# Router logits from rows not yet normed, first norm's scale and shift on gathered tokens, mixer's end in fixed order, last norm's rows from columns

## The chip, the cores and the metric

The kernel runs on one core of one Trainium2 chip. The metric is the device time of one execution in microseconds (us); the median of three executions stands for a kernel. The engines are TensorE (PE), VectorE (DVE), ScalarE (ACT), GpSimd (POOL) and SyncE (SP, which here issues nearly all transfers).

## The reference

One encoder layer over 256 tokens of width 1024. Everything is float32.

```
y  = token_mixer(x)                       # two attention branches, gates, w_out, b_out
x1 = layer_norm(ALPHA*x + y, ln1_g, ln1_b)
logits = x1 @ w_router + b_router         # 32 experts
top 4 per token, softmax over the 4 -> gates
y2[t] = sum over its 4 experts of gate * (act(x1[t] @ w_up[e] + b_up[e]) @ w_down[e] + b_down[e])
out = layer_norm(ALPHA*x1 + y2, ln2_g, ln2_b)

layer_norm(x, g, b): (x - mean) * rsqrt(var + 1e-5) * g + b
```

All 32 experts have tokens, so the 32 x 12 MB of expert weights are read once.

## The kernel before

**The mixer.** `unit(n)` and the two loops behind it go through 28 slabs of weights (w_in, w_proj_a, w_proj_b, w_out), each of 1 MB in four pieces. `split` makes a high and a low part of each piece (a cast on ACT, a subtraction on DVE or POOL), and `products` takes three matmuls of 256 columns for each 128 rows of depth. The last four slabs are those of w_out: for u = 0 to 3, PE makes columns 256u to 256u+255 of the mixer's output for two blocks of 128 tokens (tt = 0, 1), 24 matmuls each; DVE adds them to `xs` (ALPHA*x + b_out, already there) and takes `bn_stats`. In u = 3 the two token blocks go one after the other (`one_by_one`).

**Norm and router.** For each token block: mean and variance, 1/sqrt, the normed rows `nrm`, eight transposes of 128x128 into PSUM, two copies into `nT`, and eight matmuls of `wrg` (w_router with ln1_g already in it) into `lgq`, four depth groups in four groups of 32 partitions. `sums` adds the four groups into `lgp`. Beside that, POOL (block 0) and DVE (block 1) put ln1_g and ln1_b on the normed rows, which gives `x1`. Then the largest eight logits (`V.max`), the mask `s16` of the top four, the rank of each token in its expert (`rk`, `posm`), and a one-hot matrix `oh` for two experts.

**Experts.** `gather_half` multiplies `x1` with `oh` (16 matmul instructions for each half of the width) and gives the tokens of two experts, in columns, in `xe`. For expert e, `gate_of` and `up_of` (8 steps of depth each, one PSUM bank) and `down_of` run on PE, and their hooks put other small work between two steps: the gather for later experts, the transposes `turn_of`, `gates_for`, and `combine`, which adds an expert's output into the four `acc` banks. The stream of weights is g0 u0, then (g1 d0 u1), (g2 d1 u2) and so on to (g31 d30 u31), d31. Each stands for four transfers of 1 MB; they go in this order through 20 SBUF slots (`SLOTS`, the names `r_...` in the profile). SP issues the transfer into a slot when PE has used up what was there 20 transfers earlier, with at most eight on the way. In a few slots the mixer's own data lies first: `w0` and `w1` hold the split pieces, `xh` and `xl` the mixer's merged rows and later `nrm` and `nT`.

**Order.** In the mixer and the router the framework's scheduler orders each engine's instructions. From the first expert on, the order is that of the code (`manual_schedule`).

**The end.** In `up_of(31)`, four hooks spread the rows ln2_g and ln2_b over 128 partitions: ACT's queue loads the two rows into one partition (`r_tab`), a matmul of one row of depth makes `pr`, ACT copies it to `rows2` (`r_qa`). After expert 31, `final` norms `acc`: three of the four blocks on DVE, block (0, 1) on ACT and POOL, each block then written out by a transfer that SP issues in the order (0, 1), (0, 0), (1, 0), (1, 1).

## Time and profile before

| | |
|---|---|
| median of 3 runs (lowest, highest) | 1185.61 us (1184.1, 1187.65) |
| profiled execution: its time | 1182.13 us |
| its span, first to last instruction | 1180.4 us |
| PE busy | 1095.8 us, 93% |
| DVE, ACT, POOL busy | 274.1, 206.3, 55.0 us |
| moved by the DMA engines | 440.20 MB, mean 373 GB/s |
| mean granted TensorE clock | 0.98 |

The profile gives for each engine what it did when, and what released it after a wait. A matmul instruction is listed with its full latency, and the next one starts before it ends, so a busy PE isn't a PE at its peak; time per instruction in a row of matmuls is the group's time through its count. PE at 93% and DMA at 373 GB/s are means over a mixer (to about 215 us), a router (to about 232 us), 32 experts and a short end.

### The profile page before, as it was taken

What the parts mean: (1) busy time and instruction counts of PE and PEld (TensorE: products, weight loads), DVE (VectorE), ACT (ScalarE), POOL (GpSimd) and SP (SyncE); (2) the same over time, 40 slices, a digit from 0 to 9 for tenths busy, and PEclk for the clock granted to TensorE, in tenths of its full rate; (3) what the DMA queues carried; (4) which work ended last, traced back from release to release, by engine and by line L of the source; (5) the groups of instructions that cost most, each with busy time, mean ns of one, the idle gap of its engine ahead of it and who ended that gap; (6) DMA issues with size and microseconds to landing.
All of it is one profiled execution on the core that took longest, in us unless ns stands there. A gap on an engine that the chain in (4) does not pass through costs nothing.

```text
span 1180.4 us, 14053 instructions
## 1 busy us (share of the span) xinstructions
PE 1095.8 (93%) x5797; PEld 509.1 (43%) x5798; DVE 274.1 (23%) x570; ACT 206.3 (17%) x403; POOL 55.0 (5%) x77
## 2 busy tenths in 40 slices
PE   6989999799999999999999999999999899999883
PEld 6888999633334333333333333333333333333221
DVE  5957457411111111111111101111111111111103
ACT  3556654310001011010000001011000000000011
POOL 1730002200000000000000000000000000000001
PEclk9999999899999999999999989999999999999987
DMA  8765749699999999999999999999999999999971
GB/s 283 260 228 200 253 161 319 227 412 421 421 421 420 421 421 421 421 421 421 421 421 421 421 421 422 422 421 421 421 421 422 421 421 421 421 421 421 421 323 38
DMA packets 86651, 440.20 MB, mean 373 GB/s; under 512 B 7348, under 2 KB 33588, under 8 KB 37462
## 3 DMA queue, kind: packets, MB, share of 16 engines
q1 hardware_dynamic: 85666, 436.45, 91.1%
q0 software_dynamic: 720, 2.62, 0.7%
q8 instruction: 48, 0.79, 0.3%
q10 hardware_dynamic: 196, 0.17, 0.1%
q14 instruction: 21, 0.17, 0.0%
HBM read 438.16 MB, written 1.05 MB: 372 GB/s over the span
## 4 chain that ended last, share of the span: by engine, by line
DMA 56%; PE 22%; DVE 1%; issue 1%; ACT 0%; SPq 0%; ACTq 0%
DMA r_a<-in_w_ex 10%; DMA r_xl<-in_w_ex 8%; DMA r_ob<-in_w_ex 8%; DMA r_s<-in_w_ex 7%; DMA r_v<-in_w_ex 7%; PE pg L605 6%; PE pu L605 6%; DMA r_w<-in_w_ex 5%; PE pd L637 5%; DMA r_gb<-in_w_ex 3%; DMA r_qb<-in_w_ex 3%; DMA r_p<-in_w_ex 3%; PE px L581 2%; PE acc L645 1%; PE acc L681 1%
## 5 line engine op out<-in xcount | busy, mean ns | idle before, releaser
L594 DVE COPY ot<-po 128x256 f32<-128x256 f32 x32 | 13.6, 424 | 508.5 <-PE po L592 508.5
L210 PE MATMUL pt<-r_xh,r_w 128*128 128x256 f32 x512 | 101.0, 296 | 10.5 <-ACT r_w L188 5.8
L210 PEld LDWEIGHTS pt<-r_xh,r_w 128*128 128x128 f32 x512 | 84.8, 201 | 13.0 <-ACT r_w L188 5.5
L189 DVE TENSOR_TENSOR r_w<-r_s,r_w 128x512 fp32r<-128x512 f32 x104 | 72.3, 712 | 42.7 <-ACT r_w L188 42.1
L583 ACT COPY xe<-px 128x512 f32<-128x512 f32 x32 | 18.8, 586 | 356.6 <-PE px L581 349.3
L613 DVE TENSOR_SCALAR gc<-pg 128x512 f32<-128x512 f32 x32 | 22.1, 692 | 246.0 <-PE pg L605 246.0
L188 ACT CAST r_w<-r_s 128x512 fp32r<-128x512 f32 x112 | 66.8, 617 | 62.4 <-PE pt L210 31.7
L210 PE MATMUL pt<-r_xl,r_w 128*128 128x256 f32 x256 | 74.8, 292 | 0.0
L581 PEld LDWEIGHTS px<-oh,x 128*128 128x128 f32 x512 | 61.2, 196 | 28.1 <-issue 15.9
L581 PE MATMUL px<-oh,x 128*128 128x128 f32 x512 | 66.9, 285 | 1.8 <-DVE oh L572 0.9
L645 PE MATMUL acc<-y,ot 64*128 64x512 f32 x256 | 64.3, 621 | 0.7 <-ACT y L640 0.7
L640 ACT COPY y<-pd 128x512 f32<-128x512 f32 x32 | 18.8, 586 | 214.0 <-PE pd L637 214.0
L637 PE MATMUL pd<-r_a,at 128*64 128x512 f32 x224 | 51.3, 597 | 4.6 <-DMA r_a<-in_w_ex 3.9
L630 ACT COPY at<-pa 128x512 f32<-128x512 f32 x32 | 18.8, 586 | 204.5 <-PE pa L628 204.5
L605 PE MATMUL pg<-r_a,xe 128*64 128x512 f32 x224 | 53.2, 613 | 0.0
L210 PEld LDWEIGHTS pt<-r_xl,r_w 128*128 128x128 f32 x256 | 51.7, 202 | 0.1
L605 PE MATMUL pu<-r_a,xe 128*64 128x512 f32 x192 | 46.3, 603 | 2.6 <-DMA r_a<-in_w_ex 2.6
L212 PE MATMUL pt<-r_w,r_xh 128*128 128x256 f32 x256 | 47.6, 285 | 0.7 <-DVE r_w L189 0.7
L793 POOL TENSOR_TENSOR r_qb<-r_qb,r_qa 128x512 f32<-128x512 f32 x1 | 1.7, 1682 | 949.7 <-ACTq L805 949.7
L212 PEld LDWEIGHTS pt<-r_w,r_xh 128*128 128x128 f32 x256 | 40.2, 192 | 2.1 <-DVE r_w L189 1.2
L645 PEld LDWEIGHTS acc<-y,ot 64*128 64x128 f32 x256 | 22.4, 189 | 43.0 <-issue 41.4
L212 PE MATMUL pt<-r_w,r_xl 128*128 128x256 f32 x128 | 36.3, 284 | 0.2 <-DVE r_xl L490 0.2
(269 smaller groups left out, 1365.8 us busy)
## 6 DMA issues: line engine op xcount, KB each, us to landing
r_a<-in_w_ex SPq DMA_DIRECT2D x79, 1024.0 KB, 19.8
r_s<-in_w_ex SPq DMA_DIRECT2D x38, 1024.0 KB, 19.8
r_w<-in_w_ex SPq DMA_DIRECT2D x38, 1024.0 KB, 19.8
r_s<-in_w_in SPq DMA_DIRECT2D x19, 1024.0 KB, 6.5
r_qa<-in_w_ex SPq DMA_DIRECT2D x19, 1024.0 KB, 19.8
r_tab<-in_w_ex SPq DMA_DIRECT2D x19, 1024.0 KB, 19.8
r_qb<-in_w_ex SPq DMA_DIRECT2D x19, 1024.0 KB, 19.8
r_v<-in_w_ex SPq DMA_DIRECT2D x19, 1024.0 KB, 19.8
```

Source lines behind the costliest of these rows:

```text
L188: S.copy(w[:, 0:2], src)
L189: (G if n % 4 == 3 and n >= 80 else V).tensor_sub(w[:, 2:4], src, w[:, 0:2].bitcast(F32))
L210: PE.matmul(os[j], w[:, a + b, c], d[:, k], start=st, stop=sp)
L212: PE.matmul(os[j], d[:, k, c], w[:, a + b], start=st, stop=sp)
L581: PE.matmul(px[:, k], x1[:, tt, (4 * h + k) * P:(4 * h + k + 1) * P], oh[:, tt].rearrange("p a b -> p (a b)"), start=tt == 0, stop=tt == N ...
L583: S.copy(xe[:, 4 * h:4 * h + 4], px)
L605: PE.matmul(pu[h * CAP:(h + 1) * CAP], xe[:, k, i * CAP:(i + 1) * CAP], w(k)[:, h * 512:(h + 1) * 512], start=False, stop=k == KD - 1)
L613: V.tensor_scalar(gc, pg, LIMIT, None, op0=ALU.min)
L630: S.copy(at, pa)
L637: PE.matmul(pd[dh * CAP:(dh + 1) * CAP], at[:, k % 4, k // 4 * CAP:(k // 4 + 1) * CAP], w(k)[:, dh * 512:(dh + 1) * 512], start=k == 0, st ...
L640: S.copy(y, pd)
L645: PE.matmul(o, ot[q, tt], y[q], start=start, stop=stop)
```

## The change

1. **Router.** `wrg` gets its column mean subtracted over all 1024 rows (`csm`, eight more matmuls in `router_parts`), so that logits can be made from rows that aren't centred; 1/sqrt is put on the 32 logits instead of the 1024 columns. The transposes and the logit matmuls then work on `xs`, in four parts of 256 columns, each behind its unit u of w_out.
2. **First norm.** ln1_g and ln1_b no longer go on the rows: `x1` is only normed (on ACT, in place). The gathered tokens get scale and shift as columns in `gather_half`, four activations of 128x128 for one copy of 128x512. The residual for the last norm takes ALPHA*ln1_g through `spread`, and ALPHA*ln1_b as a 33rd row of `bdn`. The loads of g1 and b1 fall away.
3. **Order.** Unit u = 3 and everything to the rank stands in `manual_schedule`.
4. **Last norm.** ln2_g and ln2_b come as columns with `bcol`; they are spread in the hooks of `gate_of(31)`, one expert stage earlier, with a 128x128 identity. `final` is written in another order, and block (0, 1) goes out through ACT's queue, the others through SP's.
5. The register with the largest count is read after expert 3 instead of at the end, and the second half of the first gather uses another PSUM bank.

```diff
         def router_parts():
             ...
+            for k in range(KD):
+                PE.matmul(pl[:, 128:128 + NE], ones, wrg[:, k], start=k == 0, stop=k == KD - 1)
+            V.tensor_scalar(csm, pl[:, 128:128 + NE], -1.0 / D, None, op0=ALU.mult)
+            V.tensor_add(wrg, wrg, csm[:, None].to_broadcast([P, KD, NE]))
...
-        for u in range(4):
-            py = banks()
-            products(py, 96 + 4 * u, 4, (mh, ml), False, u == 3)
-            for tt in range(NT):
-                xq = xs[:, tt, u * 256:(u + 1) * 256]
-                V.tensor_add(xq, py[tt], xq)
-                V.bn_stats(st[:, tt, u], xq)
+        def turned_x(u, tt, xT):
+            tp = pst.tile([P, 2, P], F32, name="pt", tag="tp")
+            for j in range(2):
+                PE.transpose(tp[:, j], xs[:, tt, (2 * u + j) * P:(2 * u + j + 1) * P], ident)
+            S.copy(xT[:, tt], tp)
+        def logits(u, tt, xT):
+            for j in range(2):
+                k = 2 * u + j
+                g = slice(k % 4 * NE, (k % 4 + 1) * NE)
+                if u < 3:
+                    PE.matmul(lgq[g, tt, :P], wrg[:, k], xT[:, tt, j], start=k < 4, stop=k >= 2)
+                else:
+                    PE.matmul(lgp[:, tt], xT[:, tt, j], wrg[:, k], start=False, stop=j == 1)
+            if u == 2:
+                S.copy(lq[:, tt], lgq[:, tt, :P])
+                PE.matmul(lgp[:, tt], lq[:, tt], sums, start=True, stop=False)
+        def normed(tt):
+            ...
+                S.activation(x1[:, tt, c], xs[:, tt, c], AF.Identity, bias=nmr[:, t], scale=ri[:, t])
+        def largest(tt):
+            V.scalar_tensor_tensor(lg[:, tt], lgp[:, tt], ri[:, tt:tt + 1], lgbb, op0=ALU.mult, op1=ALU.add)
+            ...
+        for u in range(3):
+            py = banks()
+            products(py, 96 + 4 * u, 4, (mh, ml), False)
+            for tt in range(NT):
+                summed(u, tt, py)
+                turned_x(u, tt, xTs[u])
+                logits(u, tt, xTs[u])
+        with tc.manual_schedule():
+            ...
+            for i in range(4):
+                quarter(0, i)
+            summed(3, 0, py)
+            stats(0)
+            quarter(1, 0)
+            quarter(1, 1)
+            turned_x(3, 0, xTs[3])
+            normed(0)
+            quarter(1, 2)
+            logits(3, 0, xTs[3])
+            largest(0)
+            quarter(1, 3)
+            summed(3, 1, py)
+            turned_x(3, 1, xTs[3])
+            logits(3, 1, xTs[3])
+            stats(1)
+            normed(1)
+            largest(1)
...
-        S.copy(xe[:, 4 * h:4 * h + 4], px)
+        for k in range(4):
+            f = 41 + 4 * h + k
+            S.activation(xe[:, 4 * h + k], px[:, k], AF.Identity, bias=bcol[:, f + 8:f + 9], scale=bcol[:, f:f + 1])
...
+        def spread(c, m):
+            pr = ps.tile([P, 512], F32, name="pr", tag="m")
+            for k in range(4):
+                PE.matmul(pr[:, k * P:(k + 1) * P], bcol[:, c + k:c + k + 1].to_broadcast([P, P]), m, start=True, stop=True)
+            return pr
...
+                if n == NE - 1:
+                    rows2, fo = part(slot("qa"), 0, 2048, 2), part(slot("qb"), 0, 2048, 2)
+                    def rows(j, dh):
+                        S.copy(rows2[:, j, dh * 512:(dh + 1) * 512], spread(57 + 8 * j + 4 * dh, ident))
+                    for k, a in zip((1, 2, 3, 4), ((0, 0), (0, 1), (1, 0), (1, 1))):
+                        hooks[k] = lambda a=a: rows(*a)
+                gate_of(n, hooks)
...
-                        PE.matmul(pr, ones[0:1], row[:, j, c], start=True, stop=True)
-                        S.copy(rows2[:, j, c], pr)
...
-                nc.sync.dma_start(out[tt * P:(tt + 1) * P, c], o)
+                ((S if (tt, i) == (0, 1) else nc.sync)).dma_start(out[tt * P:(tt + 1) * P, c], o)
```

PE at the border between units u = 0 and u = 1 of w_out, before (`pt` is a unit's PSUM bank, `r_w_112` and `r_w_113` the split pieces, `r_xh` and `r_xl` the merged rows):

```order
L212 MATMUL pt<-r_w_113,r_xl 128x256
L212 MATMUL pt<-r_w_113,r_xh 128x256
L212 MATMUL pt<-r_w_112,r_xh 128x256
L212 MATMUL pt<-r_w_112,r_xl 128x256
L212 MATMUL pt<-r_w_112,r_xh 128x256 x2
```

PE at the same place now (`x_75` is the tile of `xs`):

```order
L211 MATMUL pt<-r_w_113,r_xh 128x256
L211 MATMUL pt<-r_w_112,r_xh 128x256
L211 MATMUL pt<-r_w_112,r_xl 128x256
L211 MATMUL pt<-r_w_112,r_xh 128x256
L495 MATMUL pt<-ident,x_75 128x128 x2
L211 MATMUL pt<-r_w_112,r_xh 128x256
L495 MATMUL pt<-ident,x_75 128x128 x2
L211 MATMUL pt<-r_w_112,r_xl 128x256
L505 MATMUL lgq<-xT,wrg 32x128 x2
L211 MATMUL pt<-r_w_112,r_xh 128x256
L505 MATMUL lgq<-xT,wrg 32x128 x2
L211 MATMUL pt<-r_w_112,r_xh 128x256
```

Between the products of u = 1 now stand the four transposes and four logit matmuls of u = 0; the same happens at the two borders that follow.

PE from the mixer's last product to the first of the rank's matmuls (L561), before:

```order
L534 MATMUL pt<-ident,nrm_2388 128x128 x8
L539 MATMUL lgq<-r_xl,wrg 32x128 x8
L534 MATMUL pt<-ident,r_xh 128x128 x8
L539 MATMUL lgq<-r_xl,wrg 32x128 x8
L549 MATMUL lgp<-sums,lq 128x32 x2
L561 LDWEIGHTS tri_135
L561 MATMUL pt<-s_2399,tri_135 128x32
```

PE at the same place now, with the mixer's last product (L211) ahead and the rank in L592:

```order
L211 MATMUL pt<-r_w_113,r_xh 128x256
L495 MATMUL pt<-ident,x_75 128x128 x2
L507 MATMUL lgq<-wrg,xT 128x32 x2
L592 LDWEIGHTS tri_134
L592 MATMUL pt<-s_2158,tri_134 128x32
```

Of 34 matmuls between the last product and the rank, four are left there.

PE in the up stage of the last expert, before (`pr` is a spread row, `acc` the sum over the experts):

```order
L605 MATMUL pu<-r_w_6225,xe 64x512 x2
L758 MATMUL pr<-r_tab,ones 128x512
L605 MATMUL pu<-r_w_6225,xe 64x512 x2
L758 MATMUL pr<-r_tab,ones 128x512
L605 MATMUL pu<-r_w_6227,xe 64x512 x2
L645 MATMUL acc_2491<-y_6218,ot 128x512
```

PE in the gate stage of the last expert now, two stages ahead of that place:

```order
L641 MATMUL pg<-r_pt,xe 64x512 x4
L725 MATMUL pr<-ident,bcol 128x128 x4
L641 MATMUL pg<-r_p,xe 64x512 x2
L725 MATMUL pr<-ident,bcol 128x128 x4
L641 MATMUL pg<-r_p,xe 64x512 x2
L725 MATMUL pr<-ident,bcol 128x128 x4
L641 MATMUL pg<-r_oa,xe 64x512 x2
L725 MATMUL pr<-ident,bcol 128x128 x4
L641 MATMUL pg<-r_oa,xe 64x512 x2
L664 MATMUL pa<-ident,uc 128x128 x4
```

The up stage of expert 31 now holds only its own products, `combine(30)` and the two transposes of `gates_for(31)`.

## Rows read from the trace of the kernel before

**Rows 1.** Page, 40 slices of the span: what the DMA engines moved.
```profile
GB/s 283 260 228 200 253 161 319 227 412 421 421 421 420 421 421 421 421 421 421 421 421 421 421 421 422 422 421 421 421 421 422 421 421 421 421 421 421 421 323 38
```
**Rows 2.** Windows, router to first expert: us, engines' busy time, clock, DMA share, GB/s.
```profile
222.00:224.00 2.00, 0.71 (x4) 0.53 (x5) 1.49 (x14) 0.00 (x0) 0.00 (x0) 0.62 1.21 377
...
228.00:230.00 2.00, 1.19 (x7) 0.92 (x7) 0.00 (x0) 0.59 (x1) 0.00 (x0) 0.67 0.00 0
...
232.00:234.00 2.00, 2.00 (x12) 0.64 (x10) 0.45 (x2) 1.41 (x4) 0.00 (x0) 1.00 0.00 0
```
**Rows 3.** Timeline from the last product: start us, us, engine, line, operation, [idle before].
```profile
214.23 0.28 PE L212 MATMUL pt<-r_w,r_xl 128*128 128x256 f32 x1
214.35 0.28 PE L212 MATMUL pt<-r_w,r_xh 128*128 128x256 f32 x1
214.67 0.42 DVE L497 TENSOR_TENSOR x<-pt,x 128x256 f32<-128x256 f32 x1
...
216.60 0.35 DVE L524 SCALAR_TENSOR_TENSOR nmr<-mv,ri 128x1 f32<-128x1 f32 x1
...
222.01 0.19 DVE L550 TENSOR_TENSOR lg<-lgp,lgbb 128x32 f32<-128x32 f32 x1 [0.29 <-PE lgp L549]
...
224.55 0.42 DVE L572 TENSOR_TENSOR oh<-io,posm 128x256 f32<-128x256 f32 x1
225.19 3.75 PE L581 MATMUL px<-oh,x 128*128 128x128 f32 x16 [0.93 <-DVE oh L572]
...
229.75 2.02 PE L581 MATMUL px<-oh,x 128*128 128x128 f32 x16 [0.81 <-ACT xe L583]
...
231.94 3.60 PE L605 MATMUL pg<-r_a,xe 128*64 128x512 f32 x16
...
233.87 2.04 SPq L123 DMA_DIRECT2D r_a<-in_w_ex  x2
```
**Rows 4.** Chain that ended last, in its last 53 us: start us, us, what.
```profile
1130.30 4.34 DMA r_tab<-in_ln_g
...
1152.70 0.70 DVE uc L621
...
1155.62 7.11 PE pd L637 x32
```
**Rows 5.** Timeline and a window: first piece of u31, and the last bytes of weights.
```profile
1130.67 1.08 PE L605 MATMUL pu<-r_w,xe 128*64 128x512 f32 x4 [0.34 <-DMA r_w<-in_w_ex]
...
1146.00:1148.00 2.00, 2.00 (x8) 0.49 (x6) 0.00 (x0) 0.59 (x1) 0.00 (x0) 1.00 0.19 78
```
**Rows 6.** Timeline of the last norm's end.
```profile
1168.72 0.78 ACT L792 ACTIVATE r_qb<-acc,nmr,rs 128x512 f32<-128x512 f32 x1 [0.29 <-DVE nmr L786]
...
1171.34 1.59 POOL L794 TENSOR_TENSOR r_qb<-r_qb,r_qa 128x512 f32<-128x512 f32 x1
...
1172.51 0.97 DVE L797 SCALAR_TENSOR_TENSOR r_qb<-r_qb,rs,r_qa 128x512 f32<-128x512 f32 x1
1172.96 2.08 SPq L798 DMA_DIRECT2D out<-r_qb  x4
```
**Rows 7.** Lines by form, 60 to 232 us: xcount, busy us, mean ns, idle before.
```profile
L353 PEld LDWEIGHTS pt<-ones,r_p 128*128 128x128 f32 x16 | 1.9, 192 | 0.0
...
L534 PE MATMUL pt<-ident,nrm 128*128 128x128 f32 x8 | 1.0, 272 | 0.0
...
L539 PE MATMUL lgq<-r_xl,wrg 128*32 128x128 f32 x32 | 1.7, 285 | 0.6 <-ACT r_xl L535 0.5
...
L344 ACT COPY ob<-pv 128x256 f32<-128x256 f32 x4 | 1.5, 374 | 2.9 <-PE pv L343 2.9
...
L548 ACT COPY lq<-lgq 128x128 f32<-128x128 f32 x2 | 0.4, 258 | 0.0
...
L583 ACT COPY xe<-px 128x512 f32<-128x512 f32 x2 | 1.2, 586 | 9.5 <-issue 7.3 <-PE px L581 2.2
```
**Rows 8.** Window in which PE runs the router's constants (L443 to L446).
```profile
152.00:154.00 2.00, 2.00 (x12) 2.00 (x11) 1.27 (x2) 0.62 (x1) 0.00 (x0) 0.50 0.91 285
```

More of the change, by code (lines that the diff above doesn't have):

```diff
@@ L517, in encoder, with stats @@
         zs = small.tile([P, NT], F32, name="zs")
-        for tt in range(NT):
+        V.memset(top, BIG)
+        def stats(tt):
             V.bn_aggr(mv[:, tt], st[:, tt].rearrange("p a b -> p (a b)"))
@@ L547, in encoder @@
-        for tt in range(NT):
-            S.copy(lq[:, tt], lgq[:, tt, :P])
-            PE.matmul(lgp[:, tt], lq[:, tt], sums, start=True, stop=True)
-            V.tensor_add(lg[:, tt], lgp[:, tt], lgbb)
-            V.max(top[:, tt], lg[:, tt])
-            V.tensor_scalar(nv1[:, tt:tt + 1], top[:, tt, 0:1], -1.0, None, op0=ALU.mult)
-            V.memset(top[:, tt, TOPK:], BIG)
+                S.activation(x1[:, tt, c], xs[:, tt, c], AF.Identity, bias=nmr[:, t], scale=ri[:, t])
+        def largest(tt):
+            V.scalar_tensor_tensor(lg[:, tt], lgp[:, tt], ri[:, tt:tt + 1], lgbb, op0=ALU.mult, op1=ALU.add)
+            t8 = small.tile([P, 8], F32, name="t8")
+            V.max(t8, lg[:, tt])
+            V.tensor_copy(top[:, tt, :TOPK], t8[:, :TOPK])
@@ new lines, in encoder, with quarter @@
+        for u in range(3):
[6 more added lines that the diff above has]
+        with tc.manual_schedule():
+            py = banks()
+            pieces = [next_piece(108 + i) for i in range(4)]
+            def quarter(tt, i):
+                products_of(py, pieces[i], i, 4, (mh, ml), False, tt)
+            for i in range(4):
[16 more added lines that the diff above has]
+            largest(1)
+            rk = pst.tile([P, 512], F32, name="pt", tag="tp")
+            for tt in range(NT):
+                o = rk[:, tt * NE:(tt + 1) * NE]
+                for t2 in range(tt):
+                    PE.matmul(o, ones16, s16[:, t2], start=t2 == 0, stop=False)
+                PE.matmul(o, tri16, s16[:, tt], start=tt == 0, stop=True)
+            V.scalar_tensor_tensor(posm.rearrange("p a b -> p (a b)"), rk[:, :NT * NE], 1.0,
+                                   s16.rearrange("p a b -> p (a b)"), op0=ALU.add, op1=ALU.mult)
+            V.tensor_scalar(nv1, top[:, :, 0], -1.0, None, op0=ALU.mult)
+            S.activation(dummy, s16[:, 1, 0:1], AF.Exp, scale=0.0)
@@ L870 @@
     a["lam"] = np.concatenate([a["lambda_q1"], a["lambda_q2"], a["lambda_k1"], a["lambda_k2"]])
-    rows = np.concatenate([a["b_in"], a["subln_g"], a["ln1_g"], a["ln1_b"]]).reshape(-1, P)
+    rows = np.concatenate([a[k] for k in ("b_in", "subln_g", "ln1_g", "ln1_b", "ln2_g", "ln2_b")]).reshape(-1, P)
     wr = a["w_router"].reshape(KD, P, NE).transpose(1, 0, 2).reshape(P, KD * NE)
```

190 lines of the change are left out of this document (80 added, 110 removed).

## Prediction

> **What bounds the kernel now.** I first read what the DMA engines move in 40 slices of the span [rows 1]: from the ninth slice (236 us; 412 GB/s) to the last but two it is 420 to 422 GB/s without a dip, and the first eight slices are far below. So from the first expert on the weight stream sets the pace, and PE, though 93% busy, only follows it. What PE does in an expert costs nothing as long as it gives slots back in time. The end is then set by two places alone: when the stream gets going, and what comes after its last bytes.
>
> **The start of the stream.** Windows of 2 us show the DMA engines at a share of 0.00 at 228 to 230 and again at 232 to 234 us [rows 2]: all 20 slots are full, and the next transfer can be issued only when PE has used the first piece of g0. The timeline gives the steps [rows 3]: last product of the mixer issued at 214.35 and ended at 214.63; one-hot matrix at 224.55; first gather half at 225.19, 3.75 us because TensorE's granted clock is 0.50 by then (0.62 in the mean of 222 to 224, 0.67 in that of 228 to 230, 1.00 at 232 [rows 2]); second half at 229.75, 2.02 us; g0 at 231.94; next transfer issued at 233.87. From the end of the last product to g0 it is 231.94 - 214.63 = 17.3 us. Whatever g0 gains, the whole stream gains.
>
> **After the stream.** The chain that ended last has PE in its last 50 us [rows 4]: at 1130.30 ACT's queue asks for the row ln2_g, which takes 4.34 us to land, and PE stands behind it in u31, with the spread matmuls. u31 ends at 1152.70 (DVE starts on it), d31 starts at 1155.62 and takes 7.11 us. But the first piece of u31 was used at 1130.67, at once on landing, and the last weights had landed by 1148 (78 GB/s are left in 1146 to 1148) [rows 5]. PE thus runs behind its data here, and only here.
>
> **The change, front.** It moves work ahead of the mixer's last product, where PE has no gap, and takes work from behind it. In units of rows 7:
> - Column mean of `wrg`: 8 matmuls, 16 instructions with 128x128 weights; 16 of such cost 1.9 us in L353. They stand beside the router's constants, where the clock is 0.50 [rows 8], so up to 3.8; I take 2.5.
> - 14 of the 16 transposes: 1.0 / 8 = 0.125 us each, 1.8 us.
> - 12 logit matmuls of 32 weight columns, 24 instructions at 1.7 / 32 = 0.053: 1.3 us.
> - 8 instructions with 128 weight columns (sums over the four groups, last logits of block 0) at 0.12: 0.9 us.
> - Waits that are new. At three borders between units PE has three products to do (0.12 us from one issue to the next [rows 3], 0.36 us) and then waits for DVE's addition, which begins 0.32 us after the last product's issue and takes 0.42 [rows 3], then for ACT's copy of the transposes, 0.37 us (L344's form) against some 0.5 us of PE work with its hops. Behind the waiting transposes and logits PE's queue holds all later products. I take 0.55 us a border, 1.6 us; bounds 0 and 3.
>
> Together the last product ends 2.5 + 1.8 + 1.3 + 0.9 + 1.6 = 8.1 us later (5.9 with no wait and the full clock, 10.8 with both worst ends).
>
> Behind the last product now lies: DVE's addition 0.04 us later, the token block's scalars 1.93 us after its start (216.60 - 214.67 [rows 3]; the two transposes, one copy and two logit matmuls fit beside that), then from logits to the one-hot matrix 224.55 - 222.01 = 2.54 us for both blocks, of which block 0's share is done earlier, so I take 2.0; the one-hot matrix and hop 225.19 - 224.55 = 0.64; the gather. Its second half no longer waits for ACT (0.81 us) as it has its own bank. The gather took 3.75 + 2.02; PE idles before it about as long as it did, so I expect part at half clock, 5.2 us (4.0 when all at full clock, 7.5 when none). Sum 0.04 + 1.93 + 2.0 + 0.64 + 5.2 + 0.1 = 9.9 us (8.7 to 12.2) against 17.3: 7.4 us less. **Net, g0 comes 8.1 - 7.4 = 0.7 us later** (from 2.8 earlier to 5.7 later). That is the surprise of this sum: work taken from behind the mixer is put into it nearly at par. The norm's row operations that POOL and DVE lose (L543 to L546) lay beside this path and give nothing.
>
> **The change, tail.** The 4.34 us wait and the spreads leave u31. In g31 there are now four spreads of 8 instructions, 4 x 8 x 0.12 = 3.8 us of PE; the copy of one (0.59 us, L583's form) is done before the next hook. A piece of 1.049 MB takes 2.49 us at 421 GB/s [rows 1], and PE uses some 1.9 for it (3.60 us for two [rows 3], and hops), so it waits at nearly each, as at 1130.67 [rows 5]; over the eight pieces of g31 and d30 it has 8 x 0.55 = 4.4 us to spare, so u31 starts within 0.3 us of its data. With pieces landing from 1130.7 on at 1133.2, 1135.6 and 1138.1, `combine(30)` (1.9 us) behind the third step: 1133.2 + 0.97 + 1.9 + 0.97 = 1137.0 for two pieces, + 1.9 for the third = 1138.9, + 2.4 with `gates_for(31)` = 1141.3. That is 1152.7 - 1141.3 = **11.4 us earlier**. d31 then starts at 1144.2 and ends at 1151.3, and its last piece, there by 1148, is used from 1149.5: the weights aren't late. Were they as late as 1150, 10.9 would remain; were the spare of g31 and d30 half of what I count, 9.5.
>
> **The last norm.** Before, SP's first output waited for POOL, which ended at 1172.93, and the four issues took 2.08 us from 1172.96 [rows 6]; DVE's last block was ready at 1173.48, but its issue was the fourth. Now DVE's three go out as they are ready, and the last is issued at about 1173.3 (relative to the old clock) instead of 1174.6; ACT's block starts with the second square root, 0.3 us before 1168.72. I take **1.5 us** (0.4 to 2.0).
>
> The Trainium skill speaks against that last step: "DMA: Bandwidth & Descriptors", section "Issuing engines are not separate DMA queues", says that transfers issued from several engines end up on the same 16 DMA engines, and that only the sequencer's issue time is saved. By it, the step would give one issue of 2.08 / 4 = 0.5 us, and the forecast would be 1.0 us higher; the trace has the order of the wait to add to it, which the rule doesn't speak of.
>
> **At nothing:** the register read after expert 3 (SP has up to eight transfers on the way); the residual's spreads at experts 17 and 19 and the wider gate row (PE's spare in the stream); four activations instead of one copy, 4 x 0.26 against 0.59 us [rows 7], since PE goes on with other steps meanwhile. If ACT's cover is gone, that costs 0.4 us for each half gather, once at g0.
>
> **Sum.** Against the profiled execution: 1182.1 + 0.7 - 11.4 - 1.5 = 1169.9 us. The median of the runs before lies 3.5 us above that execution, so 1173.4, I say 1173.5.
>
> **The rivals.**
> - *The front gains too.* No waits at the borders, full clock in the gather: 2.8 us earlier instead of 0.7 later, 1170. For it: products before overlap weight loads fully, so small matmuls between them may be partly free. Against: PE in order, and each wait stands in its queue.
> - *The clock falls at the borders.* Stretches in which PE had gaps pulled the clock to 0.50 in two places [rows 2, 8]; new waits at three borders plus the thin stretch behind the mixer could do the same. The first gather half lost 3.75 - 2.02 = 1.7 us by it [rows 3]; two such losses in the mixer and the gather wholly at half clock (7.5 instead of 5.2) are 2 x 1.7 + 2.3 = 5.7 us on top, 1179.2.
> - *The tail returns only part.* If g31's spreads block each other on the one PSUM bank and PE doesn't catch up by u31, 4 us remain there: 1177.5.
> - *Slower than before.* One mechanism: at half clock from the first border to the last product, the 24 x 2 x 3 products of 0.12 us cost 17.3 us more, 1190.8. It decides once g0 comes more than 12.9 us later, the 11.4 + 1.5 of the tail. Against: the waits that I count are under a tenth of a unit's 5.8 us.
> - *It doesn't do what it says*, that is, the rows still come late: the order shows no spread left in u31, so I give it nothing of its own.
>
> **How the numbers follow.** Forecast 0.62, front gains 0.14, clock 0.13, part of the tail 0.08, slower 0.03. The range from 1167.5 to 1180 takes in the first four nearly whole and the bounds 2.8 earlier and 5.7 later of g0. A measurement can tell 0.3%, 3.6 us, from no change, so faster means under 1182.0: all of the forecast, of the front's gain and of the tail's part, and most of the clock's case: 0.93; same 0.04; slower 0.03.
>
> **What would show it.** In the profile after: no `r_tab<-in_ln_g` in the chain; u31 without a wait beyond its pieces, DVE's `uc` about 11 us sooner after the first piece of u31 than 22.0 us; g0 within 3 us of 231.94, with the mixer's last product at about 222.7 and the DMA share still at zero for some us ahead of g0; GB/s flat at 421 after. If g0 moves by more than 5 us, my prices at the borders are wrong; if u31 ends less than 9 us earlier, the spare of g31 is.

## The result, and the profile after

The changed kernel takes 1170.53 us (median of 4 executions, 1166.54 to 1173.10) against 1184.86 us before (4 executions, 1181.37 to 1187.65): ratio 0.9878, 95% interval 0.9833 to 0.9922. In a second session it was 1172.65 us (6 executions) against 1183.89 (11): 0.9897, interval 0.9878 to 0.9916. The prediction was 1173.5 us. It was right in sum; in the front it was right for a reason that held only at equal clock.

The profiled execution of after took 1173.09 us, with a span of 1171.3. Set against the span of 1180.4 before, it divides like this (us; the marks are the first instruction of g0, DVE's first `uc` of u31, the last combine of PE, and the end of the span):

| stretch | before | after | difference | predicted |
|---|---|---|---|---|
| start to g0 | 231.94 | 236.06 | +4.1 | +0.7 |
| g0 to `uc` of u31 | 920.76 | 909.59 | -11.2 | -11.4 |
| `uc` to last combine | 10.75 | 10.75 | 0 | 0 |
| last combine to end | 16.95 | 14.90 | -2.05 | -1.5 |

The tail and the outputs came as the prediction had them. The front did not, and its 4.1 us fit this profile's place above the median: the front turned out to have more than one length (below).

**The front.** The timeline of after from the mixer's last product to g0, as in [rows 3]: start us, us, engine, line, operation, [idle before].

```profile
224.30 0.28 PE L211 MATMUL pt<-r_w,r_xh 128*128 128x256 f32 x1
224.92 0.42 DVE L514 TENSOR_TENSOR x<-pt,x 128x256 f32<-128x256 f32 x1
225.39 0.44 PE L495 MATMUL pt<-ident,x 128*128 128x128 f32 x2 [0.82 <-DVE x L514]
226.29 0.63 PE L507 MATMUL lgq<-wrg,xT 128*128 128x32 f32 x4 [0.46 <-ACT xT L496]
228.20 0.18 PE L592 MATMUL pt<-s,tri 128*128 128x32 bf16 x1 [1.24 <-DVE s L550]
229.16 6.74 PE L615 MATMUL px<-oh,x 128*128 128x128 f32 x32 [0.78 <-DVE oh L605]
...
236.06 3.60 PE L641 MATMUL pg<-r_a,xe 128*64 128x512 f32 x16
...
237.99 0.33 SPq L123 DMA_DIRECT2D r_a<-in_w_ex  x1
```

From DVE's last addition to g0 it is 236.06 - 224.92 = 11.1 us, where [rows 3] have 231.94 - 214.67 = 17.3. The gather's 32 products stand in one row now, without ACT between the halves; but they take 6.74 us. The windows say why (columns as in [rows 2]: busy time of PE, its weight loads, DVE, ACT, POOL, then clock, DMA share, GB/s):

```profile
230.00:232.00 2.00, 2.00 (x11) 2.00 (x11) 0.00 (x0) 0.00 (x0) 0.00 (x0) 0.50 1.01 426
232.00:234.00 2.00, 2.00 (x11) 2.00 (x11) 0.00 (x0) 1.02 (x3) 0.00 (x0) 0.50 1.00 422
234.00:236.00 2.00, 2.00 (x14) 1.87 (x14) 0.00 (x0) 0.55 (x3) 0.00 (x0) 0.68 0.13 53
236.00:238.00 2.00, 2.00 (x12) 0.70 (x10) 0.11 (x1) 1.85 (x6) 0.00 (x0) 1.00 0.00 0
```

The granted clock is 0.50 in the gather. The DMA engines run dry shortly after 234, ahead of g0, and stand until after 238. Further up, the timeline of PE shows a larger loss:

```profile
147.99 0.50 PE L209 MATMUL pt<-r_xh,r_w 128*128 128x256 f32 x2 [1.48 <-DVE r_w L189]
...
151.22 3.46 PE L440 MATMUL pt<-wrg,ones 128*128 128x32 f32 x16
```

and two windows the clock there:

```profile
150.00:154.00 4.00, 4.00 (x20) 4.00 (x21) 1.86 (x3) 0.00 (x0) 0.00 (x0) 0.50 0.76 248
154.00:160.00 6.00, 6.00 (x30) 6.00 (x30) 1.91 (x4) 1.71 (x3) 0.00 (x0) 0.50 0.03 10
```

PE waits 1.48 us for DVE (which waits for the output projection's bias), and the clock then stays at 0.50 from 149.9 to 160.2 us: 10.2 us, where before had 3.4 us of it, from 150.8 to 154.2, behind a wait of 1.58 us:

```profile
150.00:154.00 4.00, 4.00 (x22) 3.83 (x22) 3.16 (x7) 1.24 (x2) 0.00 (x0) 0.60 0.48 145
```

The new column mean (L440) lies inside the stretch of after and takes 3.46 us.

The borders between the mixer's last units, by contrast, show no wait at all on PE:

```profile
208.82 0.28 PE L211 MATMUL pt<-r_w,r_xh 128*128 128x256 f32 x1
208.96 0.44 PE L495 MATMUL pt<-ident,x 128*128 128x128 f32 x2
209.15 0.36 PE L211 MATMUL pt<-r_w,r_xh 128*128 128x256 f32 x1
209.35 0.38 PE L495 MATMUL pt<-ident,x 128*128 128x128 f32 x2
209.49 0.36 PE L211 MATMUL pt<-r_w,r_xl 128*128 128x256 f32 x1
209.86 0.41 PE L505 MATMUL lgq<-xT,wrg 128*32 128x128 f32 x4
210.20 0.50 PE L211 MATMUL pt<-r_w,r_xh 128*128 128x256 f32 x2
210.54 0.28 PE L211 MATMUL pt<-r_w,r_xl 128*128 128x256 f32 x1
210.75 0.41 PE L505 MATMUL lgq<-xT,wrg 128*32 128x128 f32 x4
```

No row has an idle time; the scheduler wove the transposes and logits between products of the next unit. Still a border costs time: DVE's additions for the three units start at 201.08, 208.48 and 215.88, 7.40 us apart, and before at 197.18, 202.85 and 208.61, 5.7 to 5.8 apart. So a border costs 1.6 to 1.7 us: the transposes and logits themselves, about 1.0 us by these rows, and the rest in small steps between unlike products (0.37 us from 209.49 to 209.86, where two products in a row stand 0.12 apart).

**The tail.** DVE's `uc` in the timeline:

```profile
1145.65 0.69 DVE L657 TENSOR_SCALAR uc<-pu 128x512 f32<-128x512 f32 x1 [0.59 <-PE pu L641]
```

and the chain that ended last in this stretch (start us, us, what), as in [rows 4]:

```profile
1122.23 20.87 DMA r_xl<-in_w_ex
1143.15 1.08 PE pu L641 x4
1144.60 1.03 PE pu L641 x4
1148.58 7.11 PE pd L673 x32
```

No `r_tab<-in_ln_g` any more: what u31 waits for is its last weight piece, which landed at 1143.1. From the first use of u31's weights to `uc` it is now 1145.65 - 1134.98 = 10.7 us, and 22.0 before [rows 4, 5]. In before, more than the row's load and the spreads lay in those 22.0 us:

```profile
1134.77 2.04 PE L758 MATMUL pr<-r_tab,ones 1*128 1x512 f32 x2 [3.02 <-DMA r_tab<-in_ln_g]
...
1138.00:1140.00 2.00, 2.00 (x4) 0.50 (x2) 0.00 (x0) 0.00 (x0) 0.00 (x0) 0.50 0.99 406
```

In the wait of 3.02 us for the row the granted clock fell to 0.50, from 1133.9 to 1144.1 us; u31 of after has no such stretch. The outputs, as in [rows 6]:

```profile
1163.18 1.59 POOL L839 TENSOR_TENSOR r_qb<-r_qb,r_qa 128x512 f32<-128x512 f32 x1
...
1163.68 3.46 SPq L843 DMA_DIRECT2D out<-r_qb  x3
...
1164.81 0.38 ACTq L843 DMA_DIRECT2D out<-r_qb  x1
...
1166.02 0.75 DVE L842 SCALAR_TENSOR_TENSOR r_qb<-r_qb,rs,r_qa 128x512 f32<-128x512 f32 x1
```

SP's first output leaves at 1163.68, 1.1 us before POOL's block is done.

### The profile page after: what moved, and what is told of

Same layout as the page of the kernel before. It is cut to its first block, busy times and chain, and to the rows that moved or that the text cites. A ratio compares the mean times of both kernels' runs of the same rounds, so it can differ in the third digit from the quotient of the medians.

```text
span 1171.3 us, 14250 instructions
## 1 busy us (share of the span) xinstructions
PE 1100.1 (94%) x5853; PEld 522.7 (45%) x5854; DVE 274.2 (23%) x573; ACT 238.8 (20%) x505; POOL 47.6 (4%) x71
## 4 chain that ended last, share of the span: by engine, by line
DMA 50%; PE 44%; DVE 4%; issue 1%; ACT 1%; SPq 0%; DVEq 0%; ACTq 0%
DMA r_p<-in_w_ex 10%; DMA r_w<-in_w_ex 10%; DMA r_qb<-in_w_ex 10%; PE pt L209 9%; PE pu L641 9%; DMA r_a<-in_w_ex 8%; DMA r_gb<-in_w_ex 8%; PE pg L641 7%; PE pd L673 6%; PE pt L211 3%; PE px L615 3%; PE acc L681 3%; DMA r_xl<-in_w_ex 2%; DVE r_w L189 1%; PE sc L275 1%
## 5 line engine op out<-in xcount | busy, mean ns | idle before, releaser
L619 ACT ACTIVATE xe<-px,bcol 128x128 f32<-128x128 f32 x128 | 48.1, 456 | 355.6 <-PE px L615 355.6
L209 PE MATMUL pt<-r_xh,r_w 128*128 128x256 f32 x512 | 103.5, 300 | 8.3 <-ACT r_w L188 5.4
L209 PEld LDWEIGHTS pt<-r_xh,r_w 128*128 128x128 f32 x512 | 87.0, 206 | 11.1 <-ACT r_w L188 5.1
L211 PE MATMUL pt<-r_w,r_xh 128*128 128x256 f32 x256 | 49.8, 289 | 0.6 <-DVE r_w L189 0.6
L211 PEld LDWEIGHTS pt<-r_w,r_xh 128*128 128x128 f32 x256 | 40.6, 191 | 3.1 <-issue 1.5
L211 PE MATMUL pt<-r_w,r_xl 128*128 128x256 f32 x128 | 36.6, 286 | 0.2 <-DVE r_xl L486 0.2
```

The costliest lines, as they stand in the source:

```text
L209: PE.matmul(os[j], w[:, a + b, c], d[:, k], start=st, stop=sp)
L211: PE.matmul(os[j], d[:, k, c], w[:, a + b], start=st, stop=sp)
L619: S.activation(xe[:, 4 * h + k], px[:, k], AF.Identity, bias=bcol[:, f + 8:f + 9], scale=bcol[:, f:f + 1])
```

## The experiments

Each kernel ran beside the kernel before on the same chip; the times are medians, the ratios have their 95% interval. The runs e1 to e4 shared one chip, after_again and e5 to e7 another, e8 to e11 a third; the last four had no run of the changed kernel beside them, so they are set against it by their ratios to before. To take the first 130 us out (they differ by up to 5 us between the profiles), the table also gives the time from the products with `rq` (L354; L359 before; 135.38 in the profile of before) to g0, read from each kernel's profile.

| kernel | median (executions) | ratio to before | `rq` to g0 | half clock, 146 to 160 | DVE's last addition to g0 | g0 to end |
|---|---|---|---|---|---|---|
| before | 1182 to 1185 | 1 | 96.6 | 3.4 | 17.3 | 948.5 |
| after | 1170.53 (4) | 0.9878 | 101.6 | 10.2 | 11.1 | 935.2 |
| after_again | 1172.65 (6) | 0.9897 | 101.8 | 10.2 | 9.9 | 937.0 |
| e1_tail_alone | 1172.74 (4) | 0.9923 | 96.4 | 3.4 | 17.2 | 937.8 |
| e2_front_alone | 1180.99 (10) | 0.9993 | 101.6 | 10.2 | 11.0 | 946.7 |
| e3_old_outputs | 1170.99 (5) | 0.9919 | 95.6 | none | 9.9 | 938.5 |
| e4_late_read | 1166.85 (4) | 0.9876 | 95.8 | none | 10.4 | 937.5 |
| e5_no_mean | 1166.06 (5) | 0.9848 | 95.0 | none | 11.0 | 934.9 |
| e6_early_bias | 1168.19 (4) | 0.9872 | 94.5 | none | 10.4 | 937.2 |
| e7_no_idle | 1168.85 (4) | 0.9870 | 99.5 | 10.2 | 9.0 | 935.5 |
| e8_both | 1165.67 (6) | 0.9861 | 92.8 | none | 9.0 | 936.1 |
| e9_sum_first | 1164.71 (5) | 0.9859 | 94.5 | none | 10.4 | 936.8 |
| e10_all | 1167.72 (6) | 0.9869 | 91.5 | none | 9.0 | 938.6 |
| e11_best | 1164.56 (5) | 0.9846 | 90.8 | none | 8.2 | 935.3 |

### The tail alone

The kernel before, with the spreads from columns in g31 instead of the row loads in u31:

```
-                    for j, src in enumerate((ln2g, ln2b)):
-                        S.dma_start(row[:, j], src[None, :])
...
+                    for k, a in zip((1, 2, 3, 4), ((0, 0), (0, 1), (1, 0), (1, 1))):
+                        hooks[k] = lambda a=a: rows(*a)
+                gate_of(n, hooks)
```

> The kernel before with the tail's edit alone: the rows of the last norm spread from columns in the gate step of expert 31. The theory (all eight pieces of g31 and d30 have spare for the four spreads): g0 stays at about 232 us, no row load in the chain, DVE starts on u31 about 11 us sooner after the first piece of u31 than the 22.0 us of before, and the median falls by 11 us to about 1174. The rival (the four spreads block each other on one PSUM bank, PE has not caught up by u31): 4 us of that remain, about 1178.

Measured: 1172.74 us, ratio 0.9923 (0.9898 to 0.9948). g0 at 232.13; `uc` at 1141.08, which is 909.0 us behind g0 instead of 920.8: 11.8 us gained, as the theory has it, and nothing of the rival's 4 us. That the median fell by 9.3 and not by 11 fits what the chain shows:

```profile
1136.07 3.58 PE pu L605 x16
...
1144.00 8.81 PE pd L637 x32
```

d31 took 8.81 us instead of 7.11 [rows 4]: the clock, at 0.83 in the mean of 1140 to 1150, fell here, and 1.7 us went back. It did so in the profiles of e1, e3, e4, e6, e9 and after_again, and not in those of after, e2, e5, e7, e8, e10 and e11.

### The front alone

The changed kernel with the old tail, the old outputs and the late register read:

```
-                        S.copy(rows2[:, j, dh * 512:(dh + 1) * 512], spread(57 + 8 * j + 4 * dh, ident))
...
+                    for j, src in enumerate((ln2g, ln2b)):
+                        S.dma_start(row[:, j], src[None, :])
...
-            if e == 3:
-                most = nc.values_load(cnti[0:1, NE:NE + 1], min_val=0, max_val=T)
```

> The changed kernel with the old tail, the old output order and the late register read, so the front alone. The prediction's sum: g0 0.7 us later, the median 0.7 us above before. What the changed kernel's trace showed instead (half clock from 149.8 to 160.1 us in the mixer and in the whole gather): g0 at 236, 4.1 us later, the median 4 us above before. A third reading, that this half-clock stretch comes only in some executions: times spread over about 5 us, the median 1 us below to 1 us above before.

Measured: 1180.99 us, ratio 0.9993 (0.9968 to 1.0017): the front by itself is worth nothing that can be measured. Ten executions lie between 1176.24 and 1188.23, a spread of 12 us, where fourteen of before on the same chip span 7.5. The profiled one has g0 at 236.24 and the clock at 0.50 from 150 to 160, as the profile of after has. Of the three readings the third is the nearest: the median is 1.1 us below before. But the times spread over 12 us, not 5, and the one profile doesn't show in which stretches they part.

### The old outputs

The changed kernel with the last norm's end as before:

```
-                ((S if (tt, i) == (0, 1) else nc.sync)).dma_start(out[tt * P:(tt + 1) * P, c], o)
...
-            for b in ((0, 0), (1, 0), (1, 1), (0, 1)):
-                block(*b)
+            for tt, i in ((0, 1), (0, 0), (1, 0), (1, 1)):
...
+                nc.sync.dma_start(out[tt * P:(tt + 1) * P, c], o)
```

> The changed kernel with the old end of the last norm (old order of the blocks, all four outputs on SP with POOL's block first). The prediction's term: 1.5 us slower than the changed kernel (0.4 to 2.0), seen as the time from the last combine's start to the last output issue's end, 11.6 us as before instead of 10.7. The rule of the Trainium skill that several issuing engines save issue time alone (DMA: Bandwidth & Descriptors, Issuing engines are not separate DMA queues): 0.5 us slower.

Measured: 1170.99 us, ratio 0.9919 (0.9891 to 0.9946). Its timeline at the end:

```profile
1159.52 1.59 POOL L841 TENSOR_TENSOR r_qb<-r_qb,r_qa 128x512 f32<-128x512 f32 x1
...
1160.68 0.97 DVE L844 SCALAR_TENSOR_TENSOR r_qb<-r_qb,rs,r_qa 128x512 f32<-128x512 f32 x1
1161.14 1.83 SPq L845 DMA_DIRECT2D out<-r_qb  x4
```

SP stands until POOL ends at 1161.11, as in [rows 6], and holds back two blocks of DVE that are ready by then; the last one, ready at 1161.65, is issued at 1162.58. By the measure of the expectation, from the last combine's start (1151.62) to the end of the last output's issue (1162.97), it is 11.35 us; in the ten profiles with the new order it is 10.7. So the order is worth 0.6 us there, not the 0.9 that was expected: DVE's last block is issued as soon as it is ready, but comes 0.3 us later itself, since one of DVE's steps takes 1.64 us in the new order. To the end of the span it is 16.35 us against 14.9 to 15.2 in the nine profiles with the new order and the early read, 1.1 to 1.4 us; half of that lies behind the last issue, and no run shows why. The rule of the Trainium skill (DMA: Bandwidth & Descriptors, Issuing engines are not separate DMA queues: several issuing engines only save the sequencer's time to start a transfer) gives 0.5 us. Up to the last issue the trace agrees with its size (0.6 us), though not by its reason: what is saved is a sequencer's wait for POOL less DVE's delay.

This profile also has the changed kernel's front, but this in its timeline:

```profile
147.37 0.51 PE L209 MATMUL pt<-r_xh,r_w 128*128 128x256 f32 x2 [1.43 <-DVE r_w L189]
150.03 1.87 PE L440 MATMUL pt<-wrg,ones 128*128 128x32 f32 x16
...
223.89 5.47 PE L615 MATMUL px<-oh,x 128*128 128x128 f32 x32 [0.78 <-DVE oh L605]
...
229.52 3.60 PE L641 MATMUL pg<-r_a,xe 128*64 128x512 f32 x16
```

and this in the window that was at 0.50 in after:

```profile
154.00:160.00 6.00, 6.00 (x52) 6.00 (x52) 2.77 (x4) 3.57 (x7) 0.00 (x0) 1.00 0.43 119
```

The same instructions, nearly the same wait of PE (1.43 us), and no fall of the clock: the column mean takes 1.87 us instead of 3.46, and g0 begins at 229.52, 6.5 us earlier than in the profile of after.

### The register read at the end

The changed kernel with `most = nc.values_load(...)` moved from behind expert 3 back to behind the outputs.

> The changed kernel with the register read back at the end of the program. The prediction gave the early read nothing: same time. The rival: the read stands behind the last outputs, and each engine's load of the register (0.5 us) lies in the chain at the end; then the time from the last output byte to the end of the span is 3.2 us as in before instead of 2.7, and the kernel 0.5 us slower.

Measured: 1166.85 us, ratio 0.9876 (0.9838 to 0.9914), in its times no loss. In the profile the last combine starts at 1151.16 and the span ends at 1166.7: 15.5 us, above the 14.9 to 15.2 of all nine with the early read. With the old outputs the early read (16.35) beats before (16.95) and e2 (16.8) too, but not e1 (16.1). By three pairs the early read is worth some 0.5 us, by the fourth it is not; that is too small to be settled here. The sign that was expected, the time behind the last output byte, can't be read, since the trace has no landing of the last output. The front of this profile is that of e3: no half-clock stretch at 146 to 160, g0 at 229.22.

### The changed kernel again

No edit, five rounds.

> The changed kernel once more, beside the three below on one chip. Theory: its time depends on whether the mixer's stretch at half clock (149.8 to 160.1 us in its first profile, absent in two kernels with the same front, whose g0 began at 229.5 and 229.2 instead of 236.1) comes in an execution; so its times spread over 5 to 8 us, in groups. The rival (the front's time is fixed and the profile of the tail differed): times within 2 us.

Measured: 1172.65 us; 1168.41, and five between 1171.25 and 1173.45. With the four of the first session (1166.54, 1167.96, 1173.09, 1173.10) that is seven of ten at 1171 to 1173.5 and three at 1166.5 to 1168.5. The profiled one, of 1173.45, has 10.2 us of half clock again, from about 147 to 158. The times come in groups, as the theory has it. The mean clock that is on record for each execution fits: 0.980 to 0.982 in the seven, 0.984 to 0.986 in the three, and 10.2 us at half clock take 5.1 / 1171 = 0.004 from the mean. But no execution of the lower group was profiled with the kernel unchanged; that they lack the stretch is concluded from e3 and e4.

### Without the column mean

The changed kernel without the eight products, the scaling and the addition:

```
-            for k in range(KD):
-                PE.matmul(pl[:, 128:128 + NE], ones, wrg[:, k], start=k == 0, stop=k == KD - 1)
-            V.tensor_scalar(csm, pl[:, 128:128 + NE], -1.0 / D, None, op0=ALU.mult)
-            V.tensor_add(wrg, wrg, csm[:, None].to_broadcast([P, KD, NE]))
```

> The changed kernel without the column mean of the router's weights (8 products, one scaling, one addition), so that the logits are those of rows whose mean is still in them. The prediction's price: 2.5 us, 1.9 at full clock, 3.8 at half. Theory A: only that, the half-clock stretch comes and goes as before, and g0 is 1.9 to 3.5 us earlier than in an execution of the changed kernel with the same clock. Theory B: the thin products keep the clock low, so that without them the stretch is at most 3.4 us as in the kernel before; then the slow executions go too and the median is 4 us or more below the changed kernel.

Measured: 1166.06 us, ratio 0.9848 (0.9828 to 0.9868), 6.6 us below after_again on the same chip, five executions within 3.8 us. The clock is 1.00 from 80 to 220 us in the profile, though PE's wait is there (1.42 us). That is what theory B expects, but it doesn't tell B from A: e3 and e4 have the mean and no stretch either. Against them, at the same clock, the way from `rq` to DVE's last addition is 84.0 us instead of 85.4 to 85.8, so 1.4 to 1.8 less, theory A's price. And an execution with the stretch would lie 3.5 us lower here than in the changed kernel, from 1167.8 us on, so the one of 1168.14 (mean clock 0.982; the others 0.983 to 0.985) may be one.

### The bias loaded early

The changed kernel with a free buffer for `bo`, and the addition that uses it tied to the second sub-norm, so that it doesn't move to another place:

```
-        bo = moe.tile([P, D], F32, name="bo", tag="y")
+        bo = moe.tile([P, D], F32, name="bo", tag="xe0")
...
+            V.tensor_scalar(alc, rq[:, 0:1], 0.0, ALPHA, op0=ALU.mult, op1=ALU.add)
...
-                V.scalar_tensor_tensor(xs[:, tt], xs[:, tt], ALPHA, bo, op0=ALU.mult, op1=ALU.add)
+                V.scalar_tensor_tensor(xs[:, tt], xs[:, tt], alc, bo, op0=ALU.mult, op1=ALU.add)
```

> The changed kernel with the output projection's bias loaded at the start into a buffer of its own (its old one, shared with the differential branch, kept the load back until 141 us), so that VectorE doesn't wait for it from 141.5 to 146.1 us and TensorE not for VectorE at 146.5 to 148.0. Theory: the idle time of 1.4 us is what lets the clock fall; without it no half-clock stretch at 150 to 160 in any execution, g0 at 228 (1.4 us before the 229.5 of the executions without the stretch), times within 2 to 3 us of each other, the median 4 us below the changed kernel. Rival (the clock falls there for another reason): 1.4 us only, and the spread of times stays.

Measured: 1168.19 us, ratio 0.9872 (0.9849 to 0.9895), 4.5 us below after_again; 1167.01 to 1170.85. PE has no wait between 140 and 152, and the windows that were at 0.50 read

```profile
150.00:154.00 4.00, 4.00 (x35) 4.00 (x35) 1.63 (x4) 1.38 (x3) 0.00 (x0) 1.00 0.64 224
154.00:160.00 6.00, 6.00 (x52) 6.00 (x51) 3.01 (x5) 3.57 (x7) 0.00 (x0) 1.00 0.53 156
```

From `rq` to g0 it is 94.5 us, 7.1 less than in the profile of after, 1.1 less than in e3. The theory's median came (4 below); the spread is 3.8 us, not 2 to 3, so the rival isn't shut out by four executions and one profile; and g0 is at 229.4, not 228. For the last there is a likely cause: the load at the start is not free. PE's third group of products with `r_pt` (L322 of the changed kernel) begins at 66.5 to 67.6 us in the four kernels with the early load (e6, e8, e10, e11) and at 64.4 to 65.6 in the eight others with the new front. A start between 20 and 130 us was not tried.

### The gaps before the gather filled

The changed kernel with 5, 3, 8 and 5 products of constants in PE's four gaps behind the last product:

```
+            def idle_work(n):
+                for _ in range(n):
+                    PE.matmul(junk[:, :P], ones, ident, start=True, stop=True)
...
             summed(3, 1, py)
+            idle_work(5)
             turned_x(3, 1, xTs[3])
+            idle_work(3)
```

> The changed kernel with 21 products of constants put into TensorE's four gaps between the mixer's last product and the gather (0.82, 0.46, 1.24 and 0.78 us). Theory: the gather's half clock (6.74 us in the changed kernel's profile, 5.5 in two others, 4.0 at full clock) comes from these gaps; filled, the gather takes 4.0 to 4.5 us and g0 begins 1 to 2.5 us earlier from the last product on (9 to 10 us instead of 11.5). Rival: such products don't change the granted clock, or stand in the path themselves: 11.5 us or more.

Measured: 1168.85 us, ratio 0.9870 (0.9847 to 0.9893), 3.8 us below after_again. The timeline:

```profile
223.30 1.28 PE L569 MATMUL pt<-ident,ones 128*128 128x128 f32 x10
224.41 0.38 PE L495 MATMUL pt<-ident,x 128*128 128x128 f32 x2
...
228.87 3.74 PE L625 MATMUL px<-oh,x 128*128 128x128 f32 x32
```

The gather takes 3.74 us, all at full clock; the addition stands 9.0 us ahead of g0 instead of 9.9 to 11.1. The fill was twice as long as meant: a product of this kind is two instructions, so 5 of them took 1.1 us in a gap of 0.82. The mixer's stretch at half clock is in this profile, as the table shows.

### Both edits together

> The changed kernel with both edits that held the clock: the output bias loaded at the start (no stall of TensorE at 146.5 us) and 21 products of constants in the gaps before the gather. Theory: no half-clock stretch from 80 us to the end of the gather in any execution; g0 at 229.4 - 2.0 = 227.4; times within 2 to 3 us, median 1166, some 2 us below either edit alone. Rival (the clock that is saved in one place is lost in another): g0 at 229 or later and times as for one edit, 1168 to 1169.

Measured: 1165.67 us, ratio 0.9861 (0.9838 to 0.9884), 1163.52 to 1168.24. In the profile the clock is 1.00 in the whole front, g0 starts at 225.72, and `rq` to g0 takes 92.8 us. From `rq` to g0 the gains add up; in the ratios to before (0.9861 against 0.9872 and 0.9870) the gain over one edit is inside the intervals. The spread of 4.7 us is not explained by the one profile. Of the other places in which the clock comes and goes, 60 to 80 us is at 1.00 here.

### The column mean by one product

```
-            for k in range(KD):
-                PE.matmul(pl[:, 128:128 + NE], ones, wrg[:, k], start=k == 0, stop=k == KD - 1)
+            V.tensor_reduce(wsum, wrg.rearrange("p k e -> p e k"), axis=mybir.AxisListType.X, op=ALU.add)
+            PE.matmul(pl[:, 128:128 + NE], ones, wsum, start=True, stop=True)
```

> The changed kernel with the column mean's eight products replaced by one: VectorE adds the eight chunks first (one reduction of 128x256). It computes the same. Theory A (the products' price alone): TensorE's stretch for the mean is 0.23 us instead of 1.9 (3.3 at half clock), so g0 is 1.6 to 3 us earlier and the median 1.6 to 3 us below the changed kernel, 1169 to 1171. Theory B (the thin products decide whether the clock falls): in addition no half-clock stretch at 148 to 160, as in the kernel without the mean; g0 at 228 and the median 5 us below, 1167.

Measured: 1164.71 us, ratio 0.9859 (0.9833 to 0.9884), 1164.38 to 1167.35. The timeline, and a window:

```profile
144.75 0.50 PE L209 MATMUL pt<-r_xh,r_w 128*128 128x256 f32 x2 [1.37 <-DVE r_w L189]
...
147.40 0.30 PE L441 MATMUL pt<-wsum,ones 128*128 128x32 f32 x2
...
146.00:154.00 8.00, 8.00 (x67) 7.83 (x66) 5.71 (x10) 4.02 (x8) 0.00 (x0) 1.00 0.50 139
154.00:160.00 6.00, 6.00 (x53) 6.00 (x52) 2.77 (x4) 3.57 (x7) 0.00 (x0) 1.00 0.54 187
```

0.30 us for the mean, the wait of 1.37 us is there, and the clock is 1.00 from 146 to 160. DVE's reduction (0.60 us at 26.8 us) delays nothing that PE waits for. By the ratios the median is 0.2 to 0.4% below the changed kernel's two, some 2 to 4.5 us, between the theories. With e5 that makes ten executions without the eight products, none above 1168.2. With them, seven of ten of the changed kernel lie at 1171 or more, and three of nine in e3 and e4. But without the products' own price the upper group lies 3.2 to 3.5 us lower, and before is 1.8 us faster on this chip than on that of after_again; so 1168.14 of e5 and 1166.70 and 1167.35 here may belong to it. Theory B is thus not shown. That the mean's thin products, in the place behind the wait, lengthen the stretch (before, without them, has 3.4 us of it) remains a conjecture.

It has a rival in the wait itself. In the six profiles with a stretch at half clock PE's wait ahead of it is 1.47 to 1.62 us (before and e1 among them), in the four that have the wait and no stretch (e3, e4, e5, e9) 1.35 to 1.43, as the bias took 4.77 to 4.92 us to land in the six and 4.65 to 4.72 in the four. The four profiles without the wait (e6, e8, e10, e11) have no stretch. No run separates the two; a wait held at one length, with the eight products and without them, would.

### All edits, and a fill in the tail

> The changed kernel with all three edits and 16 products of constants in the two gaps before the last down product (1.61 and 0.73 us), whose 32 products took 8.8 us instead of 7.1 in the executions in which the clock fell there. Theory: g0 at 227.4 - 1.6 = 225.8, the time from g0 to the end of the span 935.2 us in every execution, 1162.8 with 1.8 around the span: about 1163, against 1172 of the changed kernel. Rival (the weight stream or the slots are late once g0 comes sooner): g0 as told, but the stretch from g0 to the end longer than 936 us.

Measured: 1167.72 us, ratio 0.9869 (0.9846 to 0.9892): the rival. g0 starts at 227.45, 91.5 us behind `rq`, but the end comes 938.6 us later instead of 935.2:

```profile
1129.56 1.08 PE L655 MATMUL pu<-r_w,xe 128*64 128x512 f32 x4 [1.86 <-DMA r_w<-in_w_ex]
1130.57 3.67 PE L695 MATMUL acc<-y,ot 64*128 64x512 f32 x8
...
1139.13 2.72 PE L818 MATMUL pg<-ident,ones 128*128 128x128 f32 x22
```

The clock fell ahead of the filled gaps, behind a wait for a weight piece (the combine takes 3.67 us instead of 1.92), and the fill of 16 products, sized with half its real price, made the way from u31's last products to d31 5.2 us instead of 4.0 (e8). d31 took its 7.1 us, and more was lost than won. The rival's reason isn't shown: in e11 g0 begins at the same 227.47 us, and the end comes 935.3 us later.

### The version that beats both

Early bias, one product for the mean, and 3, 1, 4 and 3 products in the four gaps; no fill in the tail.

> The changed kernel with the bias loaded at the start, the column mean by one product, and the four gaps before the gather filled with 11 products of constants instead of 21 (one takes 0.25 us, two instructions, as the traces of the two kernels with 21 showed: there they overran the gaps by 1.6 us in all); nothing added in the tail. Theory: no half clock from 80 us to the gather's end; last product to g0 8.6 us instead of 9.4; g0 at 225.7 - 1.65 - 0.8 = 223.3 in an execution without a half-clock stretch at 60 to 70 us, 2 us later with it; 936 to 938 us from g0 to the end: 1161 to 1165, median 1163, some 9 us below the changed kernel. Rival (as in the kernel with all edits, clock or stream give it back later): g0 as told but over 938 us behind it, median 1166 or more.

Measured: 1164.56 us, ratio 0.9846 (0.9824 to 0.9868), five executions within 1.4 us; by the ratios 0.3 to 0.5%, some 4 to 6 us, below the changed kernel's two results (it is clear of the second's interval, not of the first's), and not to be told from e5, e8 and e9. The addition stands 8.2 us ahead of g0 and the gather takes 3.84 us. g0 itself came at 227.47, not at 225.3: 90.8 us behind `rq`, the shortest of all, but `rq` was as late as 136.72 (131 to 136 in the other profiles). Two things lie ahead of it: the early load, as in e6, and a half-clock stretch with a mean clock of 0.83 over 60 to 80 us; of the fourteen profiles only those of e8 and e9 have none there.

## Why the prediction came true, step by step

**The mixer's last product 8.1 us later (5.9 to 10.8).** From `rq` to DVE's last addition it is 214.67 - 135.38 = 79.3 us before. In e3, without half clock, it is 85.8, 6.5 more; but before has 3.4 us at half clock in this stretch, where products stand 0.213 us apart instead of 0.12, which is 3.4 x (1 - 0.12 / 0.213) = 1.5 us lost. At equal clock the change thus costs 8.0 us (7.7 with e4), the prediction's sum; that it fits so well is in part luck, since the mean cost 0.6 us less than taken and the three borders together about as much more. In the profile of after it is 90.4, 11.2 more, beyond the upper bound. The single terms: the mean 1.87 us at full clock and 3.46 at half (taken: 2.5, bounds 1.9 and 3.8); a border 1.6 to 1.7 us (taken: 4 transposes 0.5, 8 logit instructions 0.43, wait 0.55, so 1.5). The border's reason was wrong: PE doesn't wait there, since the products of the next unit stand between; the time goes into steps between unlike products, and a logit instruction takes 0.085 us, not 0.053.

**Last product to g0 9.9 us instead of 17.3.** 9.9 in e3 and after_again, 11.1 in after; bounds 8.7 to 12.2. The gather was 5.46 to 5.54 us in e3, e4 and after_again (taken: 5.2), 6.74 in after. The scalars and the one-hot matrix came within 0.3 us of the forecast.

**g0 0.7 us later.** This is the step that was mis-sized: not its terms, but that it has one value. From `rq` to g0 the change is +5.0 to +5.2 us (after, after_again, e2) or -0.7 to -0.9 (e3, e4); the two groups differ in whether the clock falls behind the wait at 147 us and, in after and e2, in a longer gather. The prediction had the clock as a rival at 0.13 and put the fall at the three borders, where nothing happens. Its own [rows 8], the half clock at 152 to 154 us, marked the place: the column mean was laid into a stretch that was at half clock already, and was priced as if only its own instructions would pay. What makes the clock fall there in one profile and not in another stays open.

**The tail 11.4 us.** 11.2 in after, 11.8 in e1. g31 has spare for the spreads: each takes 1.09 us (taken: 0.96), and u31's second piece is waited for again. What the sum left out is the clock, on both sides. Before had u31 at half clock for 10.2 us behind its wait for the row, so of the 11.2 us PE's wait is 3.0 (not the row's 4.34 us to land), and the rest is the spreads and what ran at half clock; the prediction named the wait and the spreads alone. Its figure held because it built the new u31 from the times at which the pieces land. Against that, d31 is 1.7 us longer in six of the thirteen profiles that have this tail or this front.

**The outputs 1.5 us.** 2.05 between the two profiles; by e3 the order gives 0.6 up to the last issue and 1.1 to 1.4 to the end of the span, from one profile. So the term was too large for the wait that it was built on: it had the last output issued 1173.3 - 1163.45 = 9.9 us after the last combine's start, and it is issued 10.4 us after it. The register read, priced at nothing, is worth some 0.5 us if anything.

**The sum.** The range of 1167.5 to 1180 holds nine of the ten executions of the changed kernel, both groups. The single value of 1173.5 lies at the upper group and 0.8 to 3 us above the medians. It rests on two steps that erred against each other: the profiled execution was forecast at 1169.9 us and took 1173.09, and 3.5 us were added for the median, where after's profile lies 2.6 above its median. The change, 12.1 us as forecast, was 14.3 us in the first session and 11.2 in the second.

## What to carry to other kernels

Work that is moved ahead of a bound engine's last product is paid there nearly at par, so moving it gains only what it gives back at the other end; it has to become less as well, as the mean did by one reduction on an idle engine. Where the clock of TensorE is seen at 0.50, look at what stands in and ahead of that stretch before adding work there, and remove the wait ahead of it first: a buffer that is shared for no need held back a load here, and freeing it gave 4.5 us against the changed kernel beside it. A queue that waits for the slowest producer first holds back all that is ready behind it; order outputs by when they are ready.

## What the hardware showed beyond that

The same front, with waits of PE of 1.35 to 1.62 us, ran the stretch behind them at half clock for some 10.2 us in four profiles and not at all in two others (e3, e4), and the way to DVE's last addition differed by 4.7 us or more; two more such places, at 60 to 72 us and in d31, came and went too. A median over few executions and one profile are then statements on different things. And DVE's second step of a block took 1.64 us at 1162.01 in the profile of after, with POOL at work on another block from 1161.84 on, and 0.75 us at 1166.02 with POOL idle; all ten profiles with the new order have the 1.64. Other such steps beside POOL took 0.75 to 0.97, so what POOL has to do with it stays open.
